# Where the seventh transform's spectra wait: three quarters of them in idle SBUF tiles, and the third product's tables requested in one piece

## The chip, the cores and the metric

The program runs on one core of a Trainium2 chip. The metric is the device time of one execution in microseconds (us), from which the median of several runs is taken. The engines are named as in the profile: PE (TensorE, matrix products), PEld (its weight loads), DVE (VectorE), ACT (ScalarE), POOL (GpSimd) and SP (SyncE, which here only requests transfers). ACT and POOL request transfers too. All transfers share the core's 16 DMA engines.

## The reference

A trunk of two layers over 2048 prompt positions and 512 sample positions of width 1024 in fp32: windowed attention with a gate, then Fourier mixing. Only the Fourier layer matters here.

```python
def fourier_layer(x, g, w_gate, w_out):
    b, s, d = x.shape
    h = rmsnorm(x, g)
    hg = h.astype(jnp.float32).reshape(b, s, N_FGROUPS, FGROUP_CH)
    f = jnp.fft.fftn(hg, axes=(1, 3), norm="ortho").real
    f = f.reshape(b, s, d).astype(x.dtype)
    gate = h @ w_gate
    return x + (f * jax.nn.silu(gate)) @ w_out
```

Its result goes through a last `rmsnorm` and out.

## The kernel before, in words

Every fp32 operand of a matrix product is kept as two parts, a rounded high part and the low remainder. `halves_of` makes them for one half (512 columns) of a spectrum tile: ACT casts the high part (L1423), DVE subtracts it to get the low part (L1424). `matmul3` (L117) multiplies high by high, high by low and low by high into one PSUM bank.

The transform over the prompt's 2048 positions is split into 16 residues `k1`. Residues `k1` and `16-k1` are done together, as one step that works on two spectrum tiles, a real and an imaginary one, each 128 by 1024 numbers (512 KB). The spectra of k1 = 1, 7, 3 and 5 come out of one butterfly of sums and differences on DVE (`pm` and `tt`, L1268), all at the same place in the program, while PE is busy with the output products `fo` of earlier steps. The spectra of k1 = 1 are used first and stay in SBUF (`g1r`, `g1s`). The six tiles of k1 = 7, 3 and 5 are written to memory by ACT's queue (tensors `god`, L1846) and read back by SP's queue (tiles `go`, L1863) when the step before theirs has turned its result, in four pieces of 256 KB.

From k1 = 6 on, the program runs the class `Outs`, one stage for each step. `products` of one stage does the seven output products of the step that came before it (banks `Wo`, `Zo` and `Xo` on PE, with the matrices `wo`, `fT` and `fN`), and between them, as hooks, the next step's work: `split_g` makes the parts of its spectra (tiles `gp`), `transform` multiplies them by the table `tbp` into the banks `ABp`, DVE and ACT combine these into the tiles `up` (L1461 to L1471), and PE turns `up` (`tw`, L95). A stage thus lies between two groups of turns. The rows of the residual stream (tiles `x`, read from `x1d` at L1499) get the products added (L1592), are normalised (ACT's sum of squares L1056, DVE L110, POOL's power L111, DVE's scaling L1488) and written out (L1490).

The matrices `fT` for the first two products and `s2p`, the gate, are requested by SP too. Those of the third product, `fT3`, are requested in `split_g` of the stage in which k1 = 1 is transformed, and the fourth, `fN4`, in `transform` of the same stage.

A scheduler places the instructions on each engine; anchors (`after`, `seq`) fix some orders. SP, ACT and POOL each take their requests in order, so that a request which waits holds up all that stand behind it. The SBUF tiles of this phase come from the tags `L` (20 tiles), `R` (16), `x` (4) and `hT` (8). Tag `xr` (3 tiles of 128 by 512) holds the gate's temporary tiles `gt` until the gates are done.

Of the kernel before, what the change touches and what calls it, by code (L numbers as in the profile page):

```python
# [9 lines left out]
F32 = mybir.dt.float32  # L10
# [9 lines left out]
P = 128  # L20
# [17 lines left out]
def f32(ap):  # L38
    return ap.bitcast(F32)
# [3 lines left out]
def encoder(  # L43
# [3 lines left out]
    PE, ACT, DVE, POOL, SP = nc.tensor, nc.scalar, nc.vector, nc.gpsimd, nc.sync  # L47

    cpool = ctx.enter_context(tc.tile_pool(name="cpool", bufs=1))
    main = ctx.enter_context(tc.tile_pool(name="main", bufs=1))  # L50
# [23 lines left out]
    god = {k1: [dram.tile([P, D], F32, name=f"god{k1}_{i}") for i in range(2)] for k1 in (7, 3, 5)}  # L74
# [89 lines left out]
    def seq(engine, ins):  # L164

        after(ins, chain.get(engine))
        chain[engine] = ins
        return ins
# [822 lines left out]
    def fourier_phase(tail):  # L991
        with ExitStack() as es:
# [10 lines left out]
            def right(shape, dtype, name):  # L1003
                return zp.tile(shape, dtype, align_bytes=LINE, tag="R", bufs=16, name=name)
# [3 lines left out]
            def zt(name):  # L1008
                return right([P, D], F32, name)
# [257 lines left out]
            def tt(out, a, b, op):  # L1267
                DVE.tensor_tensor(out, a, b, op)  # L1268
# [126 lines left out]
            def table(name, tab, place):  # L1395
                tb = place([P, 6, P], F32R, f"tb{name}")
                POOL.dma_start(tb.rearrange("p a c -> p (a c)"), tabs[tab])
                return tb

            def gated(name, r, place):  # L1400

                s2 = place([P, D], F32, f"s2{name}_{r[0]}")
                src, off = (s2d[0], 0) if r[0] < SEQ else (s2d[1], SEQ)
                if r[2] is None:
                    after(SP.dma_start(s2, rows(src, (r[0] - off, r[1]))), last_read[0])
                else:
                    at = bass.IndirectOffsetOnAxis(ap=mir[:, r[2] : r[2] + 1], axis=0)
                    POOL.indirect_dma_start(s2, None, src, at)
                return s2
# [4 lines left out]
            def halves_of(name, gr, gs, hf, after_one=None):  # L1414

                out = []
                for i, g in enumerate((gr, gs)):
                    if i and after_one:
                        after_one()
                    if g is not None:  # L1420
                        t = main.tile([P, 2, 512], F32R, align_bytes=LINE, tag="hT", bufs=8, name=f"g{name}_{hf}_{i}")
                        gv = g[:, hf * 512 : hf * 512 + 512]
                        ACT.copy(t[:, 0], gv)  # L1423
                        low = DVE.tensor_tensor(t[:, 1], gv, f32(t[:, 0]), ALU.subtract)  # L1424
                        if chain.get("steps"):
                            seq("dve", low)
                        out.append(t)
                return out

            last_b, last_read, gated_by = [None], [None], []  # L1430

            def position(name, tab, gr, gs, tiles, loads=None, parts=None, between=None, later=None):
# [5 lines left out]
                for hf in range(2):  # L1438
                    if hf and between:
                        between()  # L1440
                    ts = parts[hf] if parts and parts[hf] else halves_of(name, gr, gs, hf)

                    def acc(out, tabs, c0, n):
# [36 lines left out]
            def norm(x2, r, *fixed):  # L1480

                def placed(key, ins):
                    return seq(key, ins) if key in fixed else ins

                inv = sumsq(x2, f"f{r[0]}", placed)

                def scaled():
                    ins = placed("dve", DVE.scalar_tensor_tensor(x2, x2, inv[:, 0:1], gfb, ALU.mult, ALU.mult))  # L1488
                    after(ins, last_b[0])
                    after(SP.dma_start(out_rows(r), x2), last_read[0])  # L1490

                return scaled
# [34 lines left out]
            class Outs:  # L1527
# [6 lines left out]
                def turns(self):  # L1534
                    for i, v in enumerate(half_turns([u for u, r in self.us])):
                        for hf in range(2):
                            src = v[:, 4 * hf : 4 * hf + 4]
                            self.ps[i, hf] = src[:, :, ::-1, ::-1] if self.us[i][1][2] is not None else src
# [146 lines left out]
            def f_sums(w, place):  # L1685
                for k in range(4):
                    t = place([P, 2, 512], F32R, f"f{w}_{k}")
                    SP.dma_start(f32(t), f32(ftd[w][k]))
                    ft[w].append((t[:, 0], t[:, 1]))

            def pair(k1, R, base):

                if k1 == 0 or 2 * k1 == R:
                    return [(base + k1, R, None)]
                return [(base + k1, R, None), (base + R - k1, R, k1 if R == 16 else 0)]
# [81 lines left out]
            for i, l in enumerate((w0, w2)):  # L1777
                for a in range(3):
                    t = zt(f"ev{a}_{i}")
# [3 lines left out]
            A, S = ALU.add, ALU.subtract  # L1783

            def pm(a, b, name):

                n = zt(name)
                tt(n, a, b, A)
                tt(a, a, b, S)
                return n, a  # L1790
# [5 lines left out]
            f, g4s = pm(w0[1], w0[3], "f0")  # L1796
# [16 lines left out]
            for a in range(4):  # L1813
                for i, l in enumerate((pc, qs)):
# [3 lines left out]
                    t = zt(f"od{a}_{i}")  # L1818
# [14 lines left out]
            e0c, e1c = pm(tcs[0], tcs[2], "e0c")  # L1833
            o0c, o1c = pm(tcs[1], tcs[3], "o0c")
            e0s, e1s = pm(tsn[0], tsn[2], "e0s")
            o0s, o1s = pm(tsn[1], tsn[3], "o0s")
            g1r, g7r = pm(e0c, o0c, "g1r")
            g1s, g7s = pm(o0s, e0s, "g1s")
            p6 = [halves_of("p6", *G[6], 0), None]
            g3r, g5r = pm(e1c, o1s, "g3r")  # L1840
            p6[1] = halves_of("p6", *G[6], 1)
            g5s, g3s = pm(o1c, e1s, "g5s")
            G[1], G[7], G[3], G[5] = (g1r, g1s), (g7r, g7s), (g3r, g3s), (g5r, g5s)
            for k1 in (7, 3, 5):
                for t, g in zip(god[k1], G[k1]):
                    ACT.dma_start(t, g)  # L1846
            o = Outs(6, position("p6", 6, *G[6], pair(6, 16, 0), None, p6))
# [8 lines left out]

            def reads(k1):

                gl = [zt(f"go{k1}_{i}") for i in range(2)]
                for hf in range(2):  # L1860
                    cs = slice(hf * 512, hf * 512 + 512)
                    for g, src in zip(gl, god[k1]):
                        last_read[0] = SP.dma_start(g[:, cs], src[:, cs])  # L1863
                return gl, table(f"p{k1}", k1, left)

            nxt = {"r": (G[1], table("p1", 1, left))}
            for k1, k2 in ((1, 7), (7, 3), (3, 5), (5, None)):
                name, tiles = f"p{k1}", pair(k1, 16, 0)
                gl, tb = nxt["r"]

                def split_g():

                    nxt["s"] = [gated(name, r, place) for r, place in zip(tiles, (xtile, left))]
                    xb, r, whole = late[0]
                    nxt["p"] = [halves_of(name, *gl, 0, whole)]
                    if not whole:
                        o.lower()
                    o.halve(3)
                    scaled = norm(xb, r, "dve")
                    o.own(1, 1)  # L1880
                    nxt["p"].append(halves_of(name, *gl, 1))
                    scaled()
                    if not ft["T3"]:
                        f_sums("T3", right)

                def transform(third):
                    if not ft["N4"]:
                        f_sums("N4", left)
                    nxt["o"] = Outs(k1, position(name, k1, *gl, tiles, (nxt["s"], tb), nxt["p"], third))

                def turns():
                    nxt["o"].operands()
                    nxt["o"].load()
                    if k2:
                        nxt["r"] = reads(k2)

                late[0] = o.products((split_g, transform, turns, lambda: nxt["o"].others()))
                o = nxt["o"]
            def old():
# [6 lines left out]


    fourier_phase(attention_phase())


# [96 lines left out]
```

## Time and profile before

| what | value |
|---|---|
| median of three runs | 1575.81 us (1575.69 to 1577.49) |
| the profiled execution | 1575.53 us, its span 1573.5 us |
| instructions | 27706 |
| granted TensorE clock, mean | 0.999 |
| PE busy | 1561.3 us (99%) |
| DVE, ACT, POOL busy | 1169.3, 884.9, 446.3 us |
| moved by DMA | 373.91 MB, 238 GB/s in the mean |
| requests of `god` and `go` after 1380 us | 6 of 512 KB written, 12 of 256 KB read |

Times in rows of the trace are counted from the span's start. A busy PE row ends where the profile models the end of its last matmul; in a timeline the first column is a start, the second a length, and the brackets tell how long the engine was idle before it and what ended that. The part of the program that the change touches begins at about 1420 us.

### The profile page before, as it was taken

What the parts mean: (1) busy time and instruction counts of PE and PEld (TensorE: products, weight loads), DVE (VectorE), ACT (ScalarE), POOL (GpSimd) and SP (SyncE); (2) the same over time, 40 slices, a digit from 0 to 9 for tenths busy, and PEclk for the clock granted to TensorE, in tenths of its full rate; (3) what the DMA queues carried; (4) which work ended last, traced back from release to release, by engine and by line L of the source; (5) the groups of instructions that cost most, each with busy time, mean ns of one, the idle gap of its engine ahead of it and who ended that gap; (6) DMA issues with size and microseconds to landing.
All of it is one profiled execution on the core that took longest, in us unless ns stands there. A gap on an engine that the chain in (4) does not pass through costs nothing.

```text
span 1573.5 us, 27706 instructions
## 1 busy us (share of the span) xinstructions
PE 1561.3 (99%) x9818; PEld 1308.6 (83%) x9818; DVE 1169.3 (74%) x2841; ACT 884.9 (56%) x2120; POOL 446.3 (28%) x614
## 2 busy tenths in 40 slices
PE   9999999999999999999999999999999999999998
PEld 7888888888898888988888888888888888888886
DVE  5888665877548776377863577768989888989886
ACT  6788535677237774266851567646655564343353
POOL 2575652421403414124223142122121121111100
PEclk9999999999999999999999999999999999999999
DMA  8598695665865576656649665665565569557852
GB/s 290 196 331 292 230 360 208 222 238 201 294 228 197 203 267 234 242 193 237 256 150 330 229 232 195 245 250 205 211 238 199 207 235 409 182 201 285 296 195 94
DMA packets 100998, 373.91 MB, mean 238 GB/s; under 512 B 11267, under 2 KB 22283, under 8 KB 83452
## 3 DMA queue, kind: packets, MB, share of 16 engines
q1 hardware_dynamic: 83148, 298.17, 53.3%
q0 software_dynamic: 16400, 70.04, 11.4%
q10 hardware_dynamic: 1312, 3.94, 0.6%
q8 instruction: 78, 1.28, 0.3%
q14 instruction: 60, 0.49, 0.1%
HBM read 280.84 MB, written 91.26 MB: 236 GB/s over the span
## 4 chain that ended last, share of the span: by engine, by line
PE 89%; DMA 4%; DVE 3%; issue 2%; ACT 1%; POOL 0%; POOLq 0%; ACTq 0%; SPq 0%; DVEq 0%
PE gp L117 14%; PE qp L117 14%; PE spt L117 11%; PE op L117 7%; PE av L615 6%; PE spt L530 6%; PE W L117 5%; PE vp L117 3%; PE fo L117 3%; PE pt L589 3%; PE Wo L117 3%; PE Z L117 3%; PE z L1160 2%; PE Zo L117 2%; PE X L117 1%
## 5 line engine op out<-in xcount | busy, mean ns | idle before, releaser
L117 PE MATMUL gp<-h,wg 128*128 128x512 f32 x960 | 237.6, 396 | 0.0
L117 PE MATMUL qp<-h,wq 128*128 128x512 f32 x960 | 237.0, 396 | 0.0
L549 DVE CUSTOM_DVE_ANT_0 S<-spt,b 128x385 f32<-128x385 f32 (+1 forms) x320 | 156.5, 527 | 105.4 <-PE spt L530 68.3
L117 PEld LDWEIGHTS gp<-h,wg 128*128 128x128 f32 x960 | 174.9, 188 | 37.2 <-issue 1.0
L117 PEld LDWEIGHTS qp<-h,wq 128*128 128x128 f32 x960 | 174.9, 188 | 36.4 <-issue 0.2
L557 ACT ACTIVATE S<-S 128x385 f32<-128x385 f32 (+1 forms) x320 | 188.8, 596 | 19.5 <-DVE S L549 19.3
L597 ACT CAST pts<-pt 128x384 fp32r<-128x384 f32 (+1 forms) x240 | 100.6, 458 | 168.8 <-PE pt L589 160.1
L598 DVE TENSOR_TENSOR pts<-pt,pts 128x384 fp32r<-128x384 f32 (+1 forms) x240 | 114.3, 520 | 23.4 <-ACT pts L597 22.4
L639 POOL TENSOR_TENSOR uT<-o,uT 128x256 fp32r<-128x256 f32 x75 | 55.6, 741 | 229.4 <-ACT uT L638 229.3
L117 PE MATMUL spt<-wo,uT 128*128 128x512 f32 x480 | 120.4, 391 | 0.0
L117 PE MATMUL op<-wo,uT 128*128 128x512 f32 x480 | 118.9, 391 | 0.0
L530 PE MATMUL spt<-kwin,qab 64*128 64x384 f32 (+1 forms) x960 | 118.6, 353 | 0.0
L615 PEld LDWEIGHTS av<-pts,v 128*128 128x128 f32 x576 | 101.4, 188 | 18.8
L117 PE MATMUL fo<-wo,tTu 128*128 128x512 f32 x480 | 115.6, 392 | 0.2 <-ACT wo L1743 0.2
L615 PE MATMUL av<-pts,v 128*128 128x512 f32 (+1 forms) x576 | 115.7, 341 | 0.0
L117 PEld LDWEIGHTS op<-wo,uT 128*128 128x128 f32 x480 | 89.4, 188 | 18.5
L117 PEld LDWEIGHTS spt<-wo,uT 128*128 128x128 f32 x480 | 89.1, 188 | 18.3
L117 PEld LDWEIGHTS fo<-wo,tTu 128*128 128x128 f32 x480 | 88.2, 188 | 17.9 <-ACT wo L1743 0.6
L569 DVE TENSOR_SCALAR S<-S 128x384 f32<-128x384 f32 (+1 forms) x192 | 95.9, 499 | 6.8
L530 PEld LDWEIGHTS spt<-kwin,qab 64*128 64x128 f32 x960 | 74.6, 186 | 28.3 <-issue 25.7
L635 POOL TENSOR_TENSOR o<-o,s 128x256 f32<-128x256 f32 x75 | 55.4, 738 | 134.8 <-DVE o L633 134.5
L589 PEld LDWEIGHTS pt<-ident,S 64*128 64x128 f32 x1328 | 78.2, 138 | 4.5 <-issue 2.1
(337 smaller groups left out, 3210.6 us busy)
## 6 DMA issues: line engine op xcount, KB each, us to landing
wo<-wsd SPq DMA_DIRECT2D x32, 1024.0 KB, 5.7
wq<-wsd SPq DMA_DIRECT2D x31, 1024.0 KB, 7.3
wg<-wsd SPq DMA_DIRECT2D x31, 1024.0 KB, 5.8
x<-x1d SPq DMA_DIRECT2D x40, 512.0 KB, 3.7
b<-b21d SPq DMA_DIRECT2D x40, 512.0 KB, 4.7
b<-rowd SPq DMA_DIRECT2D x40, 384.0 KB, 4.1
xs<-in_x_dram SPq DMA_DIRECT2D x23, 512.0 KB, 7.4
s2d<-gt POOLq DMA_DIRECT2D x40, 256.0 KB, 4.2
```

The costliest lines, as they stand in the source:

```text
L117: ins = pe(PE.matmul(out, a[i], b[j], start=start and i + j == 0, stop=stop and i == 1, skip_group_check=more))
L530: pe(PE.matmul(banks[j][:, 2 + k0 * P : 2 + k1 * P], res["q"][rows, qp, b * P : (b + 1) * P], kwin[g][rows, kp, b * P + k0 * P : b * P + k ...
L549: seq(DVE, DVE.tensor_tensor_reduce(out=s[:, e0:e1], in0=ps[:, 1 + e0 : 1 + e1], in1=st["bias"][:, j, 386 - e1 : 386 - e0][:, ::-1], scale ...
L557: last_exp[0] = seq(ACT, ACT.activation(s[:, e0:e1], s[:, e0:e1], AF.Exp, bias=s[:, 386:387], scale=-1.0, accum_out=s[:, 387:388]))
L569: seq(DVE, DVE.tensor_scalar(s[:, ks], s[:, ks], den, None, ALU.mult))
L589: pe(PE.transpose(ps[h][:, kb, j, :], ss[j][rows, 1 + kb * P : 1 + (kb + 1) * P], ident[rows, rows]))
L597: seq(ACT, ACT.copy(hi, ps[:, k0:k1]))
L598: seq(DVE, DVE.tensor_tensor(lo, ps[:, k0:k1], f32(hi), ALU.subtract))
L615: pe(PE.matmul(to, v, pt, start=n == part == 0, stop=part == 1 and n in (1, len(todo) - 1), skip_group_check=n > 1,))
L635: eng.tensor_tensor(o, o, s, ALU.mult)
L639: low = eng.tensor_tensor(lo, o, f32(hi), ALU.subtract)
L1160: PE.matmul(to, m[part][:, g * P : (g + 1) * P], ch[:, 0, :, odd * P : (odd + 1) * P], start=part == 0, stop=part == 1,)
```

## The change

Of the two spectra of k1 = 7, the real one is computed by `half_of` into two tiles of 512 columns (`g7r0`, `g7r1`), and the lower half of the imaginary one into a third (`g7s0`); the three take tag `xr`. Only the upper half of the imaginary spectrum is still computed in place (`o0s`), written to memory and read back (`go7`), 256 KB each way. `halves_of` takes a list of halves as well as a tile. In `split_g`, the requests of the third product's matrices are placed ahead of the scaling of the rows that are just finished.

```diff
-                        gv = g[:, hf * 512 : hf * 512 + 512]
+                        gv = g[hf] if isinstance(g, list) else g[:, hf * 512 : hf * 512 + 512]
...
-            g1r, g7r = pm(e0c, o0c, "g1r")
-            g1s, g7s = pm(o0s, e0s, "g1s")
+            lower_half, upper_half = slice(0, 512), slice(512, 1024)
+
+            def half_of(a, b, cs, name):
+                t = main.tile([P, 512], F32, tag="xr", bufs=3, name=name)
+                tt(t, a[:, cs], b[:, cs], S)
+                return t
+
+            g1r = zt("g1r")
+            tt(g1r, e0c, o0c, A)
+            g7r = [half_of(e0c, o0c, cs, f"g7r{i}") for i, cs in enumerate((lower_half, upper_half))]
+            g1s = zt("g1s")
+            tt(g1s, o0s, e0s, A)
+            g7s = [half_of(o0s, e0s, lower_half, "g7s0")]
+            tt(o0s[:, upper_half], o0s[:, upper_half], e0s[:, upper_half], S)
...
-            for k1 in (7, 3, 5):
+            ACT.dma_start(god[7][1][:, upper_half], o0s[:, upper_half])
+            for k1 in (3, 5):
                 for t, g in zip(god[k1], G[k1]):
                     ACT.dma_start(t, g)
...
             def reads(k1):
 
+                if k1 == 7:
+                    t = zt("go7")
+                    last_read[0] = SP.dma_start(t[:, upper_half], god[7][1][:, upper_half])
+                    return [g7r, g7s + [t[:, upper_half]]], table("p7", 7, left)
...
                     nxt["p"].append(halves_of(name, *gl, 1))
-                    scaled()
                     if not ft["T3"]:
                         f_sums("T3", right)
+                    scaled()
```

What this does to the order of three queues follows; minus is the program before, plus the program after.

On DVE, at the butterfly, before. `gp6_a_b` are the low parts of k1 = 6 (half a, spectrum b), for which PE waits next; `x2_12` are finished rows, and the SCALAR_TENSOR_TENSOR scales them.

```order
L1268 TENSOR_TENSOR e0c_16438<-e0c_16438,o0c_16441 128x1024
L1518 TENSOR_TENSOR x2_12_16376<-x2_12_16376,fo12_1_16404 128x512
L1268 TENSOR_TENSOR g1s_16453<-o0s_16447,e0s_16444 128x1024
L1424 TENSOR_TENSOR gp6_0_0_16456<-ev0_1_15686,gp6_0_0_16456 128x512
L1268 TENSOR_TENSOR o0s_16447<-o0s_16447,e0s_16444 128x1024
L110 TENSOR_SCALAR invf12_16433<-ssf12_16430 128x1
L1424 TENSOR_TENSOR gp6_0_1_16459<-ev2_1_15690,gp6_0_1_16459 128x512
L1488 SCALAR_TENSOR_TENSOR x2_12_16376<-x2_12_16376,invf12_16433,gfb_15191 128x1024
L1268 TENSOR_TENSOR g3r_16462<-od0_0_16178,od1_1_16184 128x1024
L1424 TENSOR_TENSOR gp6_1_0_16465<-ev0_1_15686,gp6_1_0_16465 128x512
```

The same place after.

```order
L1268 TENSOR_TENSOR g7r0_16452<-e0c_16438,o0c_16441 128x512
L1268 TENSOR_TENSOR g7r1_16454<-e0c_16438,o0c_16441 128x512
L1518 TENSOR_TENSOR x2_12_16376<-x2_12_16376,fo12_1_16404 128x512
L1268 TENSOR_TENSOR g1s_16456<-o0s_16447,e0s_16444 128x1024
L1268 TENSOR_TENSOR g7s0_16458<-o0s_16447,e0s_16444 128x512
L110 TENSOR_SCALAR invf12_16433<-ssf12_16430 128x1
L1268 TENSOR_TENSOR o0s_16447<-o0s_16447,e0s_16444 128x512
L1488 SCALAR_TENSOR_TENSOR x2_12_16376<-x2_12_16376,invf12_16433,gfb_15191 128x1024
L1424 TENSOR_TENSOR gp6_0_0_16461<-ev0_1_15686,gp6_0_0_16461 128x512
L1424 TENSOR_TENSOR gp6_0_1_16464<-ev2_1_15690,gp6_0_1_16464 128x512
L1268 TENSOR_TENSOR g3r_16467<-od0_0_16178,od1_1_16184 128x1024
L1424 TENSOR_TENSOR gp6_1_0_16470<-ev0_1_15686,gp6_1_0_16470 128x512
```

The first two low parts of k1 = 6 have moved behind the scaling of `x2_12`.

On PE, at the same place, before. `ABp6_0` and `ABp6_1` are the two halves of the sixth transform; x3 is one `matmul3`.

```order
L117 MATMUL ABp6_0_16488<-gp6_0_0_16456,tbp6_16484 128x260
L117 MATMUL ABp6_1_16507<-gp6_1_0_16465,tbp6_16484 128x260
L117 MATMUL fo2_0_16546<-wo0_15221,tTu2_0_16364 128x512 x3
L117 MATMUL fo2_0_16546<-wo1_15223,tTu2_0_16364 128x512 x3
L117 MATMUL fo2_0_16546<-wo2_15245,tTu2_0_16364 128x512 x3
L117 MATMUL fo2_0_16546<-wo3_15247,tTu2_0_16364 128x512 x2
L117 MATMUL ABp6_0_16488<-gp6_0_0_16456,tbp6_16484 128x260 x2
L117 MATMUL ABp6_0_16488<-gp6_0_1_16459,tbp6_16484 128x260
```

After.

```order
L117 MATMUL ABp6_0_16492<-gp6_0_0_16461,tbp6_16488 128x260
L117 MATMUL ABp6_1_16511<-gp6_1_0_16470,tbp6_16488 128x260
L117 MATMUL fo2_0_16550<-wo0_15221,tTu2_0_16364 128x512 x3
L117 MATMUL fo2_0_16550<-wo1_15223,tTu2_0_16364 128x512 x3
L117 MATMUL fo2_0_16550<-wo2_15245,tTu2_0_16364 128x512 x3
L117 MATMUL fo2_0_16550<-wo3_15247,tTu2_0_16364 128x512 x3
L117 MATMUL fo2_0_16550<-wo4_15269,tTu2_1_16370 128x512 x3
L117 MATMUL fo2_0_16550<-wo5_15271,tTu2_1_16370 128x512 x3
L117 MATMUL fo2_0_16550<-wo6_15352,tTu2_1_16370 128x512 x3
L117 MATMUL fo2_0_16550<-wo7_15354,tTu2_1_16370 128x512
L117 MATMUL ABp6_0_16492<-gp6_0_0_16461,tbp6_16488 128x260 x2
L117 MATMUL ABp6_0_16492<-gp6_0_1_16464,tbp6_16488 128x260
```

Before the first product that needs a low part of k1 = 6 now stand 22 matmuls of `fo`, not 11. The later ones of `ABp6` move too, and the total is the same.

On SP, in the stage that transforms k1 = 1, before.

```order
L1490 DMA out_0_dram<-x2_14_16606 128x1024
L1688 DMA fT3_3_16774<-fT3d3_145 128x1024
L1688 DMA fN4_0_16789<-fN4d0_146 128x1024
L1688 DMA fN4_1_16791<-fN4d1_147 128x1024
L1688 DMA fN4_2_16793<-fN4d2_148 128x1024
L1688 DMA fN4_3_16795<-fN4d3_149 128x1024
L1499 DMA x2_1_16936<-x1d_80 128x1024
L1499 DMA x2_15_16938<-x1d_80 128x1024
L1863 DMA go7_0_16940<-god7_0_150 128x512
L1863 DMA go7_1_16941<-god7_1_151 128x512
L1863 DMA go7_0_16940<-god7_0_150 128x512
L1863 DMA go7_1_16941<-god7_1_151 128x512
```

After.

```order
L1688 DMA fT3_3_16776<-fT3d3_145 128x1024
L1490 DMA out_0_dram<-x2_14_16610 128x1024
L1688 DMA fN4_0_16793<-fN4d0_146 128x1024
L1688 DMA fN4_1_16795<-fN4d1_147 128x1024
L1688 DMA fN4_2_16797<-fN4d2_148 128x1024
L1688 DMA fN4_3_16799<-fN4d3_149 128x1024
L1499 DMA x2_1_16940<-x1d_80 128x1024
L1499 DMA x2_15_16942<-x1d_80 128x1024
L1874 DMA go7_16944<-god7_1_151 128x512
```

The fourth request of `fT3` has passed the write of `x2_14`, and of the four reads of the seventh spectra one is left. On ACT's queue two writes of `god7` of 512 KB have become one of 256 KB, behind the sum of squares of `x2_12` instead of around it. POOL's order is unchanged.

## The prediction

> **What bounds the kernel now.** First the page: is one engine full from end to end?
>
> ```profile
> span 1573.5 us, 27706 instructions
> PE 1561.3 (99%) x9818; PEld 1308.6 (83%) x9818; DVE 1169.3 (74%) x2841; ACT 884.9 (56%) x2120; POOL 446.3 (28%) x614
> ```
>
> PE is. The change takes no matmul away, so it can only give back what PE loses in the last 150 us, where its edits lie. I looked for that loss in the chain of waits, merged in order of time.
>
> ```profile
> 1451.89 2.72 PE Wo L117 x12
> ...
> 1470.82 9.31 DMA go<-god
> ...
> 1488.32 3.01 PE Zo L117 x12
> ```
>
> From 1446 us to the last 7 us the chain leaves PE once: for the seventh spectra, 9.31 us on their way from memory. That isn't 9.31 us lost, since PE had other products. What was lost shows when three stages that do the same work (turns to turns, k1 = 7, 3 and 5) are set side by side, in the table of busy time by stretch. After the stretch and its length come PE, PEld, DVE, ACT and POOL, the clock, the DMA share and GB/s.
>
> ```profile
> 1470.03:1495.34 25.31, 24.30 (x141) 19.65 (x141) 21.06 (x36) 10.07 (x21) 2.70 (x4) 1.00 0.75 271
> 1495.34:1518.71 23.37, 23.37 (x141) 19.64 (x140) 21.07 (x36) 10.20 (x21) 2.71 (x4) 1.00 0.59 202
> 1518.71:1542.10 23.39, 23.39 (x143) 19.66 (x142) 21.06 (x36) 10.20 (x21) 1.11 (x2) 1.00 0.49 170
> ```
>
> The same work at the same clock takes 25.31 us with k1 = 7 and 23.38 with the others: 1.93 us are lost. The timeline of PE says where, and that of ACT why.
>
> ```profile
> 1480.84 0.37 PE L117 MATMUL ABp<-gp,tbp 128*128 128x260 f32 x1
> 1481.55 0.64 PE L117 MATMUL ABp<-gp,tbp 128*128 128x260 f32 x3 [0.34 <-DVE gp L1424]
> ...
> 1488.32 3.01 PE L117 MATMUL Zo<-wo,S 128*128 128x512 f32 x12 [0.57 <-DVE x L1592]
> ...
> 1506.15 0.65 PE L117 MATMUL ABp<-gp,tbp 128*128 128x260 f32 x4
> 1480.15 1.25 ACT L1423 CAST gp<-go 128x512 fp32r<-128x512 f32 x2 [3.18 <-DMA go<-god]
> ```
>
> Up to its first `ABp` the stage keeps step (1480.84 is 10.81 us after its turns, 1506.15 also). Then low parts are missing, because ACT waited 3.18 us for the reload; and as DVE stood behind them, it added `x` late, for which `Zo` waited at 1488.32.
>
> Busy columns hide half of this: in the table PE is idle for 25.31 - 24.30 = 1.01 us only, and the rest is in longer busy rows. I take starts. The Trainium skill (Perfetto Trace Analysis, "Tensor Engine Instruction (MATMUL, LD_WEIGHTS)") says that a matmul's end in a profile is computed, not observed; the same 141 matmuls, 24.30 us busy here and 23.37 there, agree. By the idle column alone the gain would be 1.0.
>
> **Part by part. The reload.** After the change three of four halves need no transfer. The fourth is asked for where four were, after the turns at 1470.1.
>
> ```profile
> go<-god SPq DMA_DIRECT2D x1, 256.0 KB, 9.3
> x<-x1d SPq DMA_DIRECT2D x1, 512.0 KB, 11.9
> 1505.21 0.62 ACT L1423 CAST gp<-go 128x512 fp32r<-128x512 f32 x1 [0.37 <-PE Wo L117]
> 1508.17 1.28 DVE L1424 TENSOR_TENSOR gp<-go,gp 128x512 fp32r<-128x512 f32 x2
> ```
>
> (The first two rows are the requests at 1470.7 and 1466.3 us, the last number the time to landing.) The first of the four pieces landed at 1480.15, and the only one left should come no later. ACT casts it fourth, 1505.21 - 1495.34 = 9.87 us after the turns, so at 1479.90; DVE wants it at the end of the row at 1508.17, 13.4 us after the turns, so at 1483.5. Even at 1480.15 it is 0.25 us late for ACT and 2.7 us early (less a 0.6 us cast) for DVE, ahead of PE. So I take the whole 1.93; between its ends, 0 and 1.93, this is nearest to the two stages without the wait. If that cover went, only the second half's products would wait.
>
> The Trainium skill (DMA: Bandwidth & Descriptors, "Anatomy of one DMA — SWDGE (gpsimd) path") puts a lone transfer at 2.0 us plus bytes by 436 GB/s. That is fitted on POOL's queue, and would make an estimated 2.6 us of a piece of 256 KB: the reload would have been in time and its removal worth nothing. The row of 9.3 us decides; the page's figure is of an idle queue.
>
> **The traffic.** 768 KB written and 768 KB read go.
>
> ```profile
> 1440.00:1460.00 20.00, 20.00 (x120) 16.50 (x119) 15.51 (x27) 9.56 (x18) 3.81 (x4) 1.00 1.00 391
> 1457.17 1.60 PE L117 MATMUL ABp<-gp,tbp 128*128 128x260 f32 x12
> 1458.76 3.06 PE L117 MATMUL Wo<-fT,S 128*128 128x512 f32 x12
> 1461.66 1.60 PE L117 MATMUL ABp<-gp,tbp 128*128 128x260 f32 x12
> 1463.10 2.92 PE L117 MATMUL Zo<-wo,S 128*128 128x512 f32 x12
> 1458.02 0.69 DVE L1592 TENSOR_TENSOR x<-x,Wo 128x512 f32<-128x512 f32 x1 [3.01 <-DMA x<-x1d]
> ```
>
> The DMA engines are full from 1440 us on (share 1.00), at 391 GB/s, where 0.79 MB is 2.0 us. That delays the rows `x`, and through DVE's 3.01 us wait, PE: the first `ABp` group takes 1458.76 - 1457.17 = 1.59 us from start to start against 1.44 for the next, and `Wo` 2.90 against 2.72 for the `Wo` in the chain: 0.33 lost. The writes of `god7` lie at 1425 to 1429, before the full stretch, so they free it only by letting `x_12` out and the `fT` loads in some 1 us earlier. 0.15 of the 0.33 needs less than that; I take 0.25, between 0 and 0.33.
>
> **The butterfly.** Here the change adds a wait. DVE and PE before:
>
> ```profile
> 1424.13 1.22 DVE L1268 TENSOR_TENSOR e0c<-e0c,o0c 128x1024 f32<-128x1024 f32 x1
> 1425.26 0.68 DVE L1518 TENSOR_TENSOR x<-x,fo 128x512 f32<-128x512 f32 x1
> 1425.86 1.22 DVE L1268 TENSOR_TENSOR g1s<-o0s,e0s 128x1024 f32<-128x1024 f32 x1
> 1427.00 0.68 DVE L1424 TENSOR_TENSOR gp<-ev,gp 128x512 fp32r<-128x512 f32 x1
> ...
> 1428.73 0.15 DVE L110 TENSOR_SCALAR invf<-ssf 128x1 f32<-128x1 f32 x1
> ...
> 1429.92 1.28 DVE L1488 SCALAR_TENSOR_TENSOR x<-x,invf,gfb 128x1024 f32<-128x1024 f32 x1 [0.45 <-POOL invf L111]
> 1431.12 1.22 DVE L1268 TENSOR_TENSOR g3r<-od,od 128x1024 f32<-128x1024 f32 x1
> 1424.82 2.70 PE L117 MATMUL fo<-wo,tTu 128*128 128x512 f32 x11
> 1427.73 0.63 PE L117 MATMUL ABp<-gp,tbp 128*128 128x260 f32 x3 [0.22 <-DVE gp L1424]
> 1428.20 1.55 PE L117 MATMUL fo<-wo,tTu 128*128 128x512 f32 x6
> 1429.60 1.16 PE L117 MATMUL ABp<-gp,tbp 128*128 128x260 f32 x8
> 1430.60 2.23 PE L117 MATMUL fo<-wo,tTu 128*128 128x512 f32 x9
> 1433.00 0.63 PE L117 MATMUL ABp<-gp,tbp 128*128 128x260 f32 x3 [0.17 <-DVE gp L1424]
> ```
>
> From start to start DVE needs 1.13 for 1024 columns and 0.60 for 512, so a halved operation costs 0.07 more; the scaling takes 1.20, and begins 1.19 after its TENSOR_SCALAR, for it waits for POOL. In the new order, from 1424.13: two halves of `g7r` to 1425.33, `x_12` to 1425.93, `g1s` to 1427.07, `g7s0` to 1427.67, TENSOR_SCALAR, `o0s` to 1428.34; the scaling begins at 1427.67 + 1.19 = 1428.86 and ends at 1430.06, then the first low part is ready at 1430.06 + 0.68 = 1430.74. Queued behind the scaling, thus waiting for POOL with it, are now the low parts, and PE behind those. A `fo` matmul takes (1429.60 - 1428.20) / 6 = 0.233. PE gets to its first low part after 22 of them, at 1424.82 + 5.13 = 1429.95, and loses 0.84 with 0.05 for the signal. Before it lost 2.91 - 11 x 0.233 = 0.35 and, at 1433.00, 2.40 - 9 x 0.233 = 0.30. That second loss goes: `gp6_1_0` follows the first low part by 0.60 + 0.60 + 1.13 and is ready at 1433.07, while PE comes to it at 1433.4. Net 0.84 - 0.65 = 0.2 us slower. The wait for POOL varies:
>
> ```profile
> 1442.73 0.14 DVE L110 TENSOR_SCALAR invf<-ssf 128x1 f32<-128x1 f32 x1
> ...
> 1444.51 1.28 DVE L1488 SCALAR_TENSOR_TENSOR x<-x,invf,gfb 128x1024 f32<-128x1024 f32 x1 [0.44 <-POOL invf L111]
> ```
>
> With 1.78 (1444.51 - 1442.73) in place of 1.19 it is 0.8 slower; without any wait the scaling would begin behind `o0s` at 1428.34, 0.5 earlier, and it is 0.3 faster. I take the wait of this place.
>
> **At nothing:** the three `xr` tiles, whose last use is the store of `gt`, 106 us before 1425; ACT's dropped request; the fourth `fT3`, now ahead of a write instead of behind it. (The row of `gt` has the first and last start.)
>
> ```profile
> L1208 POOL DMA_DIRECT2D s2d<-gt x40: 539/547/584, 1087.9 to 1318.6; - x40
> ```
>
> The fourth `fT3` is used behind the turns at 1470, from where PE keeps step until `ABp`; so it was in time already, and if its own buffer made it wait on SP, the write and `fN4` behind it would wait too, which is part of the first rival.
>
> **The sum:** -1.93 - 0.25 + 0.2 = -2.0 us. On the profiled execution's 1575.53 that is 1573.5; on the median, 0.28 higher, 1573.8, which I forecast. Its own range goes from all losses gone (1.93 + 0.33 + 0.3, 1573.2) to 0.8 lost at the butterfly and no gain in traffic (1.1 faster, 1574.7).
>
> **The rivals.** *Another transfer takes the reload's place.* `x_1`, asked for at 1466.31, landed 11.9 us later at 1478.2; its addition stands on DVE before the seventh low parts and ran at 1479.04, so 0.8 us to spare. Should it or the last piece land 2 to 3 us later, the stage keeps its 25.31 us: 1575.81 + 0.2 - 0.25 = 1575.8. For it speaks the full stretch; against it that 768 KB fewer stand in it. Chance 0.12.
>
> *Only the idle column comes back,* 1.0 instead of 1.93: 1575.81 - 1.0 - 0.25 + 0.2 = 1574.8. For it, that `Zo`'s loss is DVE's order; against it the two equal stages. Chance 0.10.
>
> *Slower: the scaling holds the butterfly.* Each microsecond by which it starts later than forecast holds the low parts of k1 = 6, then PE, a microsecond. It decides from 2.0 us on; a start 4 us late would give 1577.8, and above 5.1 it would be slower by over 0.2%. For it: ACT's sum, DVE, POOL and DVE stand in one chain before PE. Against it: 1.78 is the longest of the waits above, 0.6 over the forecast. Chance 0.07.
>
> *The change doesn't do what it says* can't be in the order of requests: three of the reads are gone from it.
>
> **How the numbers follow.** The forecast has 0.71. 0.2%, or 3.15 us, is about what a measurement of this kernel can tell from no change. All losses found add up to 1.93 + 0.33 + 0.65 = 2.9 us, so faster by over 0.2% needs a loss that I did not see or the spread of the runs (1.8 us among three): 0.10, out of the forecast's share. Slower by over 0.2%: 0.05, most of the third rival. Within: 0.85. The range goes from 2.9 us and a little spread below the median, 1572.7, to the first rival and the same spread, 1576.1.
>
> **What would show it.** Right: 23.4 us between the turns of the k1 = 7 stage; no wait of ACT's `gp` for `go`; `Wo` in the stage before at 2.7; a PE wait of 0.6 at `ABp6`, none at the second. Wrong: a stage of over 25 us, and then DVE's row `x<-x,Wo` or ACT's last `gp` waiting for a transfer; or a PE wait of over 2 us near 1430.

## The result, and the profile after

| | before | after |
|---|---|---|
| median | 1575.66 us (1573.82 to 1577.67, 22 runs) | 1572.87 us (1571.32 to 1577.01, 22 runs) |
| ratio | | 0.9984, 95% interval 0.9978 to 0.9990 |
| span of the profiled execution | 1573.5 us | 1572.3 us |

The kernel is 2.8 us faster; the interval of the ratio is worth 1.6 to 3.5 us. The forecast was 1573.8. The page of the changed kernel, its first two lines:

```profile
span 1572.3 us, 27695 instructions
PE 1558.6 (99%) x9818; PEld 1308.3 (83%) x9818; DVE 1168.7 (74%) x2843; ACT 884.0 (56%) x2120; POOL 446.0 (28%) x614
```

PE does the same 9818 matmuls and is the bound as before. Where it lost less is seen in the table of busy time by stretch, here for the stage ahead of the k1 = 7 stage, that stage, and the next.

```profile
1446.00:1470.72 24.72, 24.72 (x147) 20.77 (x146) 20.50 (x35) 8.92 (x19) 3.51 (x5) 1.00 1.02 392
1470.72:1494.10 23.38, 23.38 (x141) 19.65 (x140) 21.08 (x36) 10.09 (x21) 2.69 (x4) 1.00 0.67 239
1494.10:1517.50 23.40, 23.40 (x142) 19.65 (x142) 21.08 (x36) 10.19 (x21) 2.72 (x4) 1.00 0.58 193
```

The k1 = 7 stage went from 25.31 to 23.38 us and is now like its neighbour. The stage ahead of it went from 25.03 (1445.00 to 1470.03) to 24.72. The chain of waits from 1436 to 1500 us, by line, has PE alone in it; the 9.31 us of the reload are gone from it:

```profile
by line: PE Wo L117 34.9%; PE fo L117 23.4%; PE Zo L117 17.8%; PE ABp L117 10.5%; PE Xo L117 8.5%; PE tw L95 5.3%
```

PE's timeline after:

```profile
1425.75 5.19 PE L117 MATMUL fo<-wo,tTu 128*128 128x512 f32 x22
1431.73 0.63 PE L117 MATMUL ABp<-gp,tbp 128*128 128x260 f32 x3 [0.79 <-DVE gp L1424]
...
1458.16 1.61 PE L117 MATMUL ABp<-gp,tbp 128*128 128x260 f32 x12
1459.61 2.91 PE L117 MATMUL Wo<-fT,S 128*128 128x512 f32 x12
1462.36 1.61 PE L117 MATMUL ABp<-gp,tbp 128*128 128x260 f32 x12
...
1481.53 0.65 PE L117 MATMUL ABp<-gp,tbp 128*128 128x260 f32 x4
...
1487.18 2.91 PE L117 MATMUL Zo<-wo,S 128*128 128x512 f32 x12
```

The waits at 1481.55 and 1488.32 have no counterpart any more. One wait stands where two stood at the sixth transform, before the first product that needs a low part. From the first `ABp` of that transform to its turns it is 20.49 us (1425.51 to 1446.00) against 20.42 before (1424.58 to 1445.00). ACT's casts of the seventh spectra, after:

```profile
1477.57 0.62 ACT L1423 CAST gp<-g7r 128x512 fp32r<-128x512 f32 x1
1478.09 0.62 ACT L1423 CAST gp<-g7s 128x512 fp32r<-128x512 f32 x1
...
1479.61 0.63 ACT L1423 CAST gp<-g7r 128x512 fp32r<-128x512 f32 x1
1480.60 0.62 ACT L1423 CAST gp<-go 128x512 fp32r<-128x512 f32 x1 [0.36 <-PE Wo L117]
```

None waits for a transfer. The fourth, the only one of a reloaded piece, waited for PE. DVE after, at the butterfly and in the stage before:

```profile
1428.59 0.15 DVE L110 TENSOR_SCALAR invf<-ssf 128x1 f32<-128x1 f32 x1
...
1429.79 1.28 DVE L1488 SCALAR_TENSOR_TENSOR x<-x,invf,gfb 128x1024 f32<-128x1024 f32 x1 [0.44 <-POOL invf L111]
1430.99 1.29 DVE L1424 TENSOR_TENSOR gp<-ev,gp 128x512 fp32r<-128x512 f32 x2
...
1458.65 0.69 DVE L1592 TENSOR_TENSOR x<-x,Wo 128x512 f32<-128x512 f32 x1 [3.08 <-DMA x<-x1d]
```

The scaling begins 1.20 us after its TENSOR_SCALAR, and the low parts stand right behind it. The last row still waits for `x_6`, now until 12.65 us after the turns at 1446.00, before until 13.02 us after those at 1445.00.

From the first `ABp` of the sixth transform to the end the two profiles differ by +0.07 - 0.31 - 1.93 = -2.2 us by these starts. The spans differ by 1.2 only, because the changed profile came to that `ABp` 0.93 us later (1425.51 against 1424.58); a second profile of the kernel before came to it at 1425.41, so that this is no effect of the change.

### The profile page after: what moved, and what is told of

Read it like the earlier page. It is cut to its first block, busy times and chain, and to the rows that moved or that the text cites. A ratio compares the mean times of both kernels' runs of the same rounds, so it can differ in the third digit from the quotient of the medians.

```text
span 1572.3 us, 27695 instructions
## 1 busy us (share of the span) xinstructions
PE 1558.6 (99%) x9818; PEld 1308.3 (83%) x9818; DVE 1168.7 (74%) x2843; ACT 884.0 (56%) x2120; POOL 446.0 (28%) x614
## 4 chain that ended last, share of the span: by engine, by line
PE 89%; DVE 4%; issue 3%; DMA 2%; ACT 1%; POOL 0%; SPq 0%; POOLq 0%; ACTq 0%; DVEq 0%
PE gp L117 14%; PE qp L117 14%; PE spt L117 11%; PE op L117 7%; PE av L615 6%; PE spt L530 6%; PE W L117 5%; PE vp L117 3%; PE Wo L117 3%; PE fo L117 3%; PE pt L589 3%; PE Z L117 3%; PE Zo L117 2%; PE z L1160 1%; PE X L117 1%
```

## The experiments

The first set takes the change apart. *Spectra only:* the requests stay where they were (diffs are against the changed kernel, unless said otherwise; every ratio is to the kernel before as timed beside it).

```diff
+                    scaled()
                     if not ft["T3"]:
                         f_sums("T3", right)
-                    scaled()
```

> Only the spectra are kept in SBUF; the third product's matrices are requested as before, with the scaling ahead of the fourth of them. If the reload's wait is the whole matter, the k1 = 7 stage (turns to turns) takes 23.4 us, the stage before it 24.7, the time is 2.0 to 2.8 us under the kernel before. If the order of the requests brings a part, the stage before it comes back to 25.0 us, or the k1 = 7 stage is over 23.6.

Measured: 1573.44 us, ratio 0.9987 (0.9978 to 0.9996). *Order only:* the spectra go through memory as before, and only the third product's requests move (diff against the kernel before).

```diff
-                    scaled()
                     if not ft["T3"]:
                         f_sums("T3", right)
+                    scaled()
```

> The kernel before with the order of the requests alone changed (fourth fT3 ahead of the write of x2_14), all four halves of the seventh spectra still through memory. If the reload's wait is the whole matter: k1 = 7 stage 25.3 us, stage before it 25.0, time within 0.5 us of before. If asking for the matrices together is worth something, one of the two stages is shorter by more than 0.2 us.

Measured: 1574.98 us, ratio 0.9997 (0.9988 to 1.0005). The two intervals overlap, but the stages do not: that of k1 = 7 took 23.38 us with the spectra alone and 25.03 with the order alone. The time comes with the spectra. Is it the reload, or the bytes? *Traffic back* moves all the old bytes, the three writes and three reads as well, but into places that nobody reads.

```diff
+            for i, t in enumerate(g7r):
+                ACT.dma_start(god[7][0][:, i * 512 : i * 512 + 512], t)
+            ACT.dma_start(god[7][1][:, lower_half], g7s[0])
             ACT.dma_start(god[7][1][:, upper_half], o0s[:, upper_half])
...
+                    idle = zt("go7i")
+                    for dst, src, cs in ((idle, god[7][0], lower_half), (idle, god[7][0], upper_half), (t, god[7][1], lower_half)):
+                        after(SP.dma_start(dst[:, cs], src[:, cs]), last_read[0])
```

> The changed kernel, with the traffic of before put back and nobody waiting for it: the three halves kept in SBUF are also written to memory, and three reads of 256 KB follow the one that is needed, into tiles that nothing uses. If the gain is the removed wait: k1 = 7 stage 23.4 us, time 1.5 to 2.5 us under the kernel before; the stage before it may go back from 24.7 to 25.0, since the writes are in the queue ahead of its rows. If the gain is relief of the full DMA engines, the k1 = 7 stage is over 24.5 us and the time within 0.7 us of before.

Measured: 1573.66 us, ratio 0.9989 (0.9981 to 0.9998). Its stage before the k1 = 7 stage, in the table of busy time by stretch:

```profile
1446.15:1470.87 24.72, 24.72 (x147) 20.77 (x146) 20.52 (x35) 8.93 (x19) 3.51 (x5) 1.00 1.02 395
```

24.72 us, the same as without these bytes, and the k1 = 7 stage took 23.37. So the bytes cost nothing in either stage: what counts is that nobody waits for the reload.

*P6 early* puts the first two low parts of k1 = 6 ahead of the halves on DVE, to take PE's new wait away.

```diff
+            p6 = [halves_of("p6", *G[6], 0), None]
             g1r = zt("g1r")
...
-            p6 = [halves_of("p6", *G[6], 0), None]
```

> The changed kernel, with the first two low parts of k1 = 6 written ahead of the butterfly of k1 = 1 and 7, so that DVE makes them before the halves and before the scaling that waits for POOL. If PE's wait of 0.85 us at the butterfly comes from their place behind the scaling, it goes: the stretch from the first ABp of k1 = 6 to the turns goes from 20.5 to 19.8 us, 0.2 us of waiting staying at the second half, and the time is 0.6 us under the changed kernel. If DVE, which is full there, is short of time whatever the order, the wait comes back at the second half or at the turns and the stretch stays at 20.4 to 20.6.

Measured: 1572.64 us, ratio 0.9986 (0.9978 to 0.9995). PE's timeline:

```profile
1425.56 6.28 PE L117 MATMUL fo<-wo,tTu 128*128 128x512 f32 x27
1432.56 0.63 PE L117 MATMUL ABp<-gp,tbp 128*128 128x260 f32 x3 [0.71 <-DVE gp L1424]
```

The wait moved from the first half to the second, as was expected above for a DVE that is short of time; the stretch is 20.32 us instead of 20.49. *P6 both* moves the other two low parts ahead as well.

```diff
+            p6 = [halves_of("p6", *G[6], 0), None]
             g1r = zt("g1r")
             tt(g1r, e0c, o0c, A)
+            p6[1] = halves_of("p6", *G[6], 1)
...
-            p6 = [halves_of("p6", *G[6], 0), None]
...
-            p6[1] = halves_of("p6", *G[6], 1)
```

> The changed kernel, with all four low parts of k1 = 6 written ahead of the halves of k1 = 7, the first two ahead of g1r. If only their place in DVE's order makes PE wait, two short waits of 0.3 us in all stay at ABp, the stretch from the first ABp of k1 = 6 to the turns goes from 20.5 to 19.9 us, and the time is 0.6 us under the changed kernel (some 2.7 under before). If DVE is short of time there, the wait moves on to the turns, which need its rows up, and the stretch stays at 20.3 or more, as it did with two of the four moved (20.32).

Measured: 1574.54 us, ratio 0.9996 (0.9987 to 1.0005). PE's timeline, and DVE's row `x`:

```profile
1445.17 1.21 PE L95 MATMUL tw<-ident,up 64*128 64x64 f32 x32 [0.46 <-DVE up L1471]
...
1459.92 3.03 PE L117 MATMUL Wo<-fT,S 128*128 128x512 f32 x12 [0.97 <-DVE x L1592]
```

```profile
1459.17 0.69 DVE L1592 TENSOR_TENSOR x<-x,Wo 128x512 f32<-128x512 f32 x1 [3.98 <-DMA x<-x1d]
```

Both waits at the transform are gone. But the turns now wait for DVE, `x_6` lands 14.0 us after them instead of 12.65, and `Wo` waits 0.97 us for the row that uses it: this stage takes 26.03 us. The stretch at the transform is 0.2 us shorter than after the change (20.27 us), this stage 1.3 longer.

Three runs on the remaining reload. *Lower only* keeps one half of each spectrum in SBUF and reloads both upper halves.

```diff
-            g7r = [half_of(e0c, o0c, cs, f"g7r{i}") for i, cs in enumerate((lower_half, upper_half))]
+            g7r = [half_of(e0c, o0c, lower_half, "g7r0")]
+            tt(e0c[:, upper_half], e0c[:, upper_half], o0c[:, upper_half], S)
...
+                    for cs, src in zip((lower_half, upper_half), god[7]):
+                        last_read[0] = SP.dma_start(t[:, cs], src[:, upper_half])
...
```

> Only the two lower halves of the seventh spectra stay in SBUF; both upper halves (2 x 256 KB) go through memory. By the forecast's due times (DVE wants the upper halves 12.8 and 13.4 us after the turns, the lower ones at 9.6 and 10.8) two halves are enough: k1 = 7 stage 23.4 us, ACT's third cast waiting up to 1 us for its transfer. If any wait of ACT for a reload reaches PE, the stage is over 23.8.

Measured: 1573.13 us in a single run, k1 = 7 stage 23.39. By this one profile, two tiles of 512 columns would have done. *Quarter last* is traffic back (its writes are left out below) with the one read that counts placed behind the three idle ones.

```diff
-                    last_read[0] = SP.dma_start(t[:, upper_half], god[7][1][:, upper_half])
+                    for dst, src, cs in ((idle, god[7][0], lower_half), (idle, god[7][0], upper_half), (t, god[7][1], lower_half)):
+                        last_read[0] = SP.dma_start(dst[:, cs], src[:, cs])
+                    read = SP.dma_start(t[:, upper_half], god[7][1][:, upper_half])
+                    after(read, last_read[0])
...
```

> The changed kernel with all of the old traffic, and the one piece that is needed asked for last, behind three reads of 256 KB that nobody uses. If the due times hold, it may land 2 us later than in the changed kernel: ACT's last cast for k1 = 7 waits, the stage stays at 23.4 to 23.6. If it shows 24 or more, the last quarter had less to spare than the forecast says (2.1 us on DVE).

Measured: 1574.04 us in a single run. ACT's timeline:

```profile
1481.08 0.63 ACT L1423 CAST gp<-go 128x512 fp32r<-128x512 f32 x1 [0.93 <-DMA go<-god]
```

The piece came 10.4 us after the turns (at 1470.64), ACT waited 0.93 us for it, and the stage still took 23.38: the fourth quarter came 0.6 us behind ACT's due time at no cost. That is the first part of the spare time that the prediction worked out; the rest of it no run tried. *After again* is the changed kernel for a second profile.

> The changed kernel once more, for the stage before k1 = 7 (turns to turns), which took 25.03 us before, 24.72 after and 24.72 with the old traffic back, but 24.97 with the spectra alone. If the change shortens it, it is 24.7 again; if its length only follows when the rows x_6 happen to land, it can be anything from 24.7 to 25.0 and goes with the end of DVE's wait for them (12.6 us after the turns at 24.72, 13.0 at 25.03).

Measured: 1573.03 us in a single run; stages 24.78 and 23.38.

*Pool halves* lets POOL compute the three tiles, to take them off DVE, which is full at this place.

```diff
-                tt(t, a[:, cs], b[:, cs], S)
+                POOL.tensor_tensor(t, a[:, cs], b[:, cs], S)
```

> The changed kernel with one difference: POOL and not DVE computes the three 512-column tiles (g7r0, g7r1, g7s0). POOL is busy for 0.86 us between 1417.5 and 1444.0. My theory is that PE's 0.85 us at the sixth transform come from DVE's order alone: without the three subtractions (1.8 us of DVE) the two first low parts stand ahead of the scaling of x_12 and are ready near 1428, 3 us earlier, ahead of PE. The stretch from the first product of ABp6 to the turns should then go from 20.49 to about 19.65 and the rest stay (24.7 and 23.4): 0.8 us faster than the changed kernel, about 1572. Rival 1, the wait goes elsewhere, as it did when the low parts were moved ahead by hand: the turns then wait for DVE's up, or the writes of god and with them x_6 come later and the stage before grows towards 26.0; the sum is then even with the changed kernel or up to 0.5 us slower. Rival 2, POOL and DVE hinder each other while both read SBUF: DVE's rows beside POOL's get longer by up to POOL's own time (about 2.2 us), the low parts come about 1 us earlier instead of 3, and the gain is nearly the same; DVE's rows of 1.22 us would show it.

Measured: 1576.82 us, ratio to the kernel before 1.0009 (1.0000 to 1.0018), by the two ratios about 4 us above the changed kernel. The stretch from the first `ABp` to the turns is 23.54 us. POOL's, DVE's and PE's timelines, and the table of busy time for the twelve matmuls behind the wait:

```profile
1422.41 2.21 POOL L1841 TENSOR_TENSOR g7s<-o0s,e0s 128x512 f32<-128x512 f32 x1 [5.46 <-DVE o0s L1268]
```

```profile
1422.25 1.22 DVE L1268 TENSOR_TENSOR g1r<-e0c,o0c 128x1024 f32<-128x1024 f32 x1
1423.38 2.32 DVE L1268 TENSOR_TENSOR od<-od,z 128x1024 f32<-128x1024 f32 x1
1425.62 1.21 DVE L1268 TENSOR_TENSOR g1s<-o0s,e0s 128x1024 f32<-128x1024 f32 x1
...
1427.96 1.28 DVE L1424 TENSOR_TENSOR gp<-ev,gp 128x512 fp32r<-128x512 f32 x2
```

```profile
1424.13 2.25 PE L117 MATMUL fo<-wo,tTu 128*128 128x512 f32 x9
1428.69 0.87 PE L117 MATMUL ABp<-gp,tbp 128*128 128x260 f32 x3 [2.31 <-DVE gp L1424]
1429.36 0.63 PE L117 MATMUL fo<-wo,tTu 128*128 128x512 f32 x1
1429.78 1.92 PE L117 MATMUL ABp<-gp,tbp 128*128 128x260 f32 x8
1431.50 3.74 PE L117 MATMUL fo<-wo,tTu 128*128 128x512 f32 x14
```

```profile
1428.69:1431.50 2.81, 2.81 (x12) 2.72 (x13) 2.36 (x4) 0.00 (x0) 1.40 (x1) 0.54 0.32 127
```

The low parts came earlier, but not by the 3 us of my theory. In this profile the transform itself came earlier; against its first `ABp` the low parts begin 4.07 us behind it (1427.96, `ABp` at 1423.89), in the changed kernel 5.48 (1430.99 and 1425.51), so they gained 1.4 us. Rival 2 took a part of the rest: `od`, which began beside POOL's row, took 2.24 us from start to start, and `g1r` before it 1.13.

On PE's side the theory failed outright. The scheduler moved the product of the low parts forward too, behind 9 matmuls of `fo` and not 22, so PE came to it 2.5 us behind its first `ABp` and waited 2.31 us; behind 22 matmuls, 5.4 us after that `ABp`, it would have found the first of them ready (4.75 us after it, by the rows above). And a third cost that neither theory had: after the pause the granted clock was 0.54, and the twelve matmuls to 1431.50 took 2.81 us where the changed kernel needs 1.67 (1431.73 to 1433.40). In the next microsecond the clock was still 0.60, from 1432.50 on 1.00. The longer wait (1.6 us more than in the changed kernel, by the starts), the twelve matmuls (1.1) and the fourteen behind them (0.3) are about the 3.05 us by which the stretch is longer.

The last set repeats three kernels for second profiles, because one number didn't fit. What was open is why the stage before the k1 = 7 stage got shorter, if not by fewer bytes. SP's timeline showed a difference, before and then after: the row of `x_12` is written out, and the first `fT` load requested, earlier against the turns.

```profile
1431.23 0.34 SPq L1490 DMA_DIRECT2D out_dram<-x  x1
1433.88 0.32 SPq L1499 DMA_DIRECT2D x<-x1d  x1
1434.30 3.07 SPq L1688 DMA_DIRECT2D fT<-fT1d  x4
```

```profile
1431.10 0.34 SPq L1490 DMA_DIRECT2D out_dram<-x  x1
1433.71 0.32 SPq L1499 DMA_DIRECT2D x<-x1d  x1
1434.08 3.29 SPq L1688 DMA_DIRECT2D fT<-fT1d  x4
```

That is 10.70 us ahead of the turns at 1445.00, and 11.92 us ahead of those at 1446.00.

> The kernel before, unchanged, for a second profile. The stage before the k1 = 7 stage took 25.03 us in its first profile and 24.72 to 24.78 in four profiles with the changed order at the butterfly and the changed order of the requests. Theory: this follows from when the fT loads enter the DMA queues (first request 10.70 us before the turns here, 11.9 us before them there), so again 10.7 and about 25.0. Rival: it is scatter of a single profile; then the stage may come out anywhere from 24.7 to 25.1.

> The change without the moved requests, for a second profile. Its first fT load came 11.92 us before the turns, as early as in the changed kernel, but the stage took 24.97 us, like the kernel before. If the early loads were all there is to it, this profile should show 24.7 to 24.8 and 24.97 was scatter; if it is 24.9 to 25.0 again, the order of the requests has a part in it that I can't explain, since the requests that move stand behind those of x_6.

> The moved requests without the new place of the spectra, for a second profile. First fT load 10.70 us before the turns; stage 24.91 us in the first profile. By the theory of the early loads it is again 24.9 to 25.0; the k1 = 7 stage, whose reload landed 0.3 us earlier here, again about 25.0 and not 25.3. If the order of the requests had a part of its own, 24.7 to 24.8 would be possible here.

The single runs took 1575.45, 1573.68 and 1574.72 us. The profiles of the study, without the two in which the later loads changed their place too (P6 both, whose second group of `fT` loads came only 2.8 us ahead of the turns, and pool halves):

| kernel | first `fT` load, us ahead of the turns | DVE's row that waits for `x_6`, us behind the turns | stage before | k1 = 7 stage |
|---|---|---|---|---|
| before; again | 10.70; 10.71 | 13.02; 12.88 | 25.03; 24.91 | 25.31; 24.58 |
| order only; again | 10.70; 10.71 | 12.88; 12.88 | 24.91; 24.90 | 25.03; 25.22 |
| P6 early | 11.10 | 12.84 | 24.86 | 23.38 |
| spectra only; again | 11.92; 11.91 | 12.94; 12.64 | 24.97; 24.72 | 23.38; 23.38 |
| after; again | 11.92; 11.91 | 12.65; 12.76 | 24.72; 24.78 | 23.38; 23.38 |
| traffic back | 11.88 | 12.60 | 24.72 | 23.37 |
| lower only | 11.88 | 12.66 | 24.73 | 23.39 |
| quarter last | 11.88 | 12.57 | 24.72 | 23.38 |

Late loads gave 24.90 to 25.03 in four profiles of four; early loads 24.72 to 24.78 in six of seven, with or without the old bytes, with or without the moved requests. That is the theory of the early loads. No run moved these loads alone, so the link is a correlation over eight kernels and not an isolated cause.

The third column stands nearer to the cause. DVE's row begins when `x_6` has landed, and the stage is as long as this start plus 12.02 us, to 0.01 us, in each of the seven profiles in which it begins 12.76 us or more behind the turns, the odd 24.97 among them (12.94); P6 both lies on the same line (14.00 and 26.03). Up to 12.66 us the stage stays at 24.72 or 24.73. So its length follows the landing of `x_6`. Why that was late in one of the two profiles of spectra only, with its loads early, stays open. Early loads are no guarantee either: pool halves had the first one 14.8 us ahead and took 24.91 us, with DVE waiting for another row of `x`.

The last column held a surprise: the second profile of the kernel before lost less to the reload than the first.

```profile
1445.86:1470.77 24.91, 24.91 (x147) 20.89 (x147) 20.49 (x35) 8.93 (x19) 3.51 (x5) 1.00 1.00 381
1470.77:1495.35 24.58, 23.95 (x141) 19.69 (x141) 21.06 (x36) 10.07 (x21) 2.70 (x4) 1.00 0.76 269
```

The four profiles with the whole reload lost 1.93, 1.20, 1.65 and 1.84 us against 23.38, in the mean 1.65.

## Why the prediction was right, step by step

**The reload** (forecast -1.93): right, by the two profiles to the hundredth, and traffic back shows that the wait was the cause and not the bytes. But the term was read from one profile that happened to be the worst of four; 1.65 would have been the better price. That the wait was so long because the DMA engines were full is argued, not isolated; it fits that in the changed kernel the write of `o0s`, also 256 KB, was requested at 1429.38 with the DMA engines at rest and landed 2.0 us later, where the first piece of the old reload took 9.3.

**The due times.** ACT's fourth cast was forecast for 9.87 us after the turns and ran at 1480.60, 9.88 after. DVE was forecast to want the last quarter 13.4 us after the turns, 2.7 us of spare time; quarter last used up the first 0.6 of it at no cost.

**The traffic** (forecast -0.25, of 0 to -0.33): the size was right, -0.31 between the two profiles and about -0.2 in the mean of the table. Of the two reasons that stood there, one fell and one held. Fewer bytes were worth nothing. The `fT` loads "some 1 us earlier" were 1.22 us earlier, and they were so because of DVE's new order: the scaling of `x_12` ends 15.0 us ahead of the turns (1430.99) and not 13.9 (1431.12), and its write lets the loads in. With the old writes back they were as early (11.88 us ahead of the turns). So this gain belongs to the butterfly's edit and not to the reads and writes that went, and that the size came out right was luck.

**The butterfly** (forecast +0.2): PE lost 1431.73 - 1425.75 - 22 x 0.233 = 0.85 us, forecast 0.84; the second wait went, as forecast. The stretch grew by 0.07 and not by 0.2, since the kernel before lost 0.13 more in it than the two waits that I had priced: most of it, 0.09, in the three products behind its second wait, 0.46 us from start to start (1433.00 to 1433.46) against 0.37 where nothing waits (1434.33 to 1434.70 after).

**The sum:** -2.2 us by the starts, forecast -2.0. Measured were -2.8, interval -3.5 to -1.6, which holds both. The other kernels that keep the spectra in SBUF, measured beside each other, came out at -1.7 (traffic back) to -2.2 (P6 early) by their ratios, nearer to the sum. What the medians have beyond it, no row of the part that the change touches shows, and it stays open. With the prices of all profiles the sum would be -1.65 - 0.2 + 0.05 = -1.8: the forecast came as near as it did with the help of a reload that was priced too high, and the measured time lies close to the fast end of the range.

**The rivals.** Another transfer in the reload's place: no, the stage is 23.38 and ACT waits for none. The idle column alone: no, 1.93 came back between the two profiles and not 1.0. The scaling that holds the butterfly: the wait for POOL was the one of this place (1.20 us against 1.19), so it had no occasion. Pool halves and P6 both are what that rival would have looked like: when DVE or its writes come late at this place, it costs PE 1 to 3 us.

## What to carry to other kernels

Compare stages that do the same work by their starts: the difference prices a wait, while idle columns show only part of it; and read it from two profiles or more, since a wait on a full queue differs by 0.7 us from one profile to the next. Keeping data in SBUF pays by the wait that it takes away, not by its bytes: here a quarter could go on through memory, and the old bytes put back cost nothing. Taking away a wait on a full engine by reordering it, or by handing work to another engine, has to be followed to the end of the next stage: of three trials here one gained nothing that could be measured and two lost more than they won.

## What the runs showed of the hardware

**A pause of PE can cost more than its length.** In the profile of pool halves, after 2.31 us without a matmul the granted clock was 0.54 over the next 2.81 us, which cost a further 1.1 us, and 0.60 in the microsecond behind them. After the pauses of 0.79 us in the changed kernel and 0.97 us in P6 both it was 1.00. The Trainium skill (TensorE: Matmul & The Clock Gate, "HAM oscillation — how this bites in real kernels") sets the limit for such gaps at about 3.4 us. Here 2.31 was already too long, in the one profile that has such a pause, and the measurement decides.

**POOL holds up DVE on fp32 sums and differences of two tiles in SBUF.** DVE's operation `od` on 1024 columns took 2.24 us from start to start beside POOL's row; in the changed kernel, without POOL, the same operation took 1.13 (1423.92 to 1425.05). `od` began at 1423.38, and POOL's row ran from 1422.41 to 1424.62, so that 1.24 us of it were left; DVE lost 1.11, nearly all of that. The Trainium skill (Trainium Architecture — The Big Picture, "What this means for kernel authors") speaks of one port pair that the two share under an exclusive lock, and not as a split of bandwidth; the row agrees with DVE standing still until POOL is done. POOL's own row, 2.21 us for 512 columns, then holds a wait as well, since its first 0.97 us lay beside `g1r`, which lost nothing: elsewhere in the same profile POOL's operations on 512 columns (L240) took 1.35 us in the mean. DVE needs 0.60.
